# Memory attention one block behind the projections, its tail between the gates of the merge stage: a hybrid gMLP decoder layer on eight cores

## The chip, the cores and the metric

The kernel runs on all 8 cores of one Trainium2 chip: two dies of four cores, cores 0 to 3 and 4 to 7. Each core computes one prompt sequence of 2048 tokens and 16 of the 128 sample sequences (128 tokens); the cores exchange nothing. The metric is the time of the slowest core in microseconds (us). So a change helps only as far as it helps the core that ends last.

Engines as the profile names them: PE is the matrix engine, PEld its weight loads, DVE is VectorE, ACT is ScalarE, POOL is GpSimd, SP issues most DMAs. PEclk is the share of full clock that PE was granted.

## The reference, cut to what matters

```python
h = rmsnorm(x, g_mix)
u, v, p, q, gate_logits = split(h @ w_in)
vhat = layernorm(gelu(v), g_v, b_v)
a = chunk_spatial_gate(gelu(u), vhat, w_s, b_s) @ w_out_a     # within chunks of 128 tokens
b = multiscale_pool(p, ...) @ w_out_b
c = memory_attend(q, mem_k, mem_v) @ w_out_c                  # 4 heads, 256 memory tokens
g_a, g_b, g_c = split(sigmoid(gate_logits))
x = x + (g_a * a + g_b * b + g_c * c) @ w_o
x = x + square(relu(rmsnorm(x, g_ffn) @ w_up)) @ w_down
# outputs: y = rmsnorm(x, g_final), memory k and v, the pooling state, and
# the vhat rows of the last chunk (prompt) and of the sample
```

Matmul operands are bf16, sums are fp32.

## The kernel before

A small scheduler in the file records every operation with the buffers that it reads and writes, and emits each engine's instructions in the order in which they were recorded. So the order of the Python calls is the order on every engine's queue. A buffer comes from a ring; an engine that wants one waits for its last readers. There are 8 PSUM banks in one ring (`pb`), 7 tiles `fA` (`tA`), 4 tiles `fW` (`tW`), and 4 tiles each in the rings for x and for normalised x.

The front works block by block (512 tokens): `Q`, `V`, `P` are projections, `S(j, hp)` the attention scores and their Exp, `AV(j, hp)` the attention output (with Ln and Exp for the division), `WIN` the pooling windows, `U` and `MIX` the spatial gate. `T` transposes, `N` normalises, `vout(i)` writes the normalised v rows. `SA1`, `SA2`, `SA2b`, `SA3` are the same attention for a group of 4 sample sequences, each step waiting for the one before. In the kernel before, all this belongs to block `j` itself:

```python
for j in range(1, 4):
    Q(j)
    ...                                   # V(j) with norms of the next block
    S(j, 0); S(j, 1)
    if j >= 2: SA1(g0); SA1(g1)
    for i in range(4): P(BT[j][i]); vout(i)
    if j == 3: flush(); P(16); vout(4)    # token tile 16 is the sample
    if j >= 2: SA2(g0); SA2(g1)
    if j == 3: load_next("mrg1"); load_next("mrg2")
    WIN(j)
    ...                                   # SA2b, WIN(4), AV(j,0), AV(j,1), T, SA3
    us = [U(j, g) for g in range(4)]      # j == 3: U4() before
    for g in range(4): MIX(j, g, *us[g])
```

`vout(i)` writes the normalised v rows. For the last prompt tile (15) and the sample (16) they are also an output, scaled with gain and bias.

```python
if t >= 15:
    (g0, g0_b), (g1, g1_b), (g2, g2_b) = [tS(t) for _ in range(3)]
    s.dma("sp", [(g0[:], gbv[0:512].partition_broadcast(128))], ...)       # gain
    s.dma("sp", [(g1[:], gbv[512:1024].partition_broadcast(128))], ...)    # bias
    TS("dve", g2[:], gv[:], *sc, ...)
    TT("pool", g2[:], g2[:], g0[:], ALU.mult, ...)
    TT("pool", g2[:], g2[:], g1[:], ALU.add, ...)
    store([(cvo[...], g2[:])], ...)       # issued by the next flush()
```

`MIX` ends on GpSimd as well: `TT("pool", apre[...], tm, ug, mult)`. Then the merge: for each of 8 slices of 128 output channels and 5 column ranges, three gates (24 matmuls, Sigmoid), the three branch products (8 matmuls), and the sum. After it come the output projection, the MLP and the final norm; the change does not touch them.

The softmax here doesn't subtract the row's maximum and nothing guards it: scores larger than these inputs give would overflow.

Of the kernel before, what the change touches and what calls it, by code (L numbers as in the profile page):

```python
# [7 lines left out]
F32 = mybir.dt.float32  # L8
# [178 lines left out]
def build_program():  # L187
# [30 lines left out]
    with st, nc.allow_non_contiguous_dma(reason="small strided rows"), \  # L218
# [14 lines left out]
        def Xt(t):  # L233
# [26 lines left out]
        kvs = [CRf[:, i * 4096:(i + 1) * 4096] for i in range(2)]  # L260
        kvs_b = [[s.buf("kvs%d_%d" % (i, a)) for a in range(2)] for i in range(2)]
        probs = CRf[:, 8192:12288].rearrange("p (a c) -> p a c", a=8)
        probs_b = [s.buf("probs%d" % i) for i in range(8)]
        hmT = CRf[:, 8192:10240].rearrange("p (k c) -> p k c", k=8)
        hmT_b = probs_b[0:4]
        qbd = CRf[:, 12288:13312].rearrange("p (f b c) -> p f b c", f=2, b=16)
        qbd_b = s.buf("qbd")
        prt = [CRf[:, 13312 + i * 512:13824 + i * 512] for i in range(5)]
        prt_b = [s.buf("prt%d" % i) for i in range(5)]
        bnds = CRf[:, 15872:17408]  # L270
        bnds_b = s.buf("bnds")
        cr_old = [(i * 4096 + a * 2048, i * 4096 + a * 2048 + 2048, kvs_b[i][a]) for i in range(2) for a in range(2)] + \
                 [(8192 + i * 512, 8704 + i * 512, probs_b[i]) for i in range(8)] + [(12288, 13312, qbd_b)] + \
                 [(13312 + i * 512, 13824 + i * 512, prt_b[i]) for i in range(5)] + [(15872, 17408, bnds_b)]
# [133 lines left out]
        def norm_load(t, src):  # L408
            xt, xb = ring("xst", xst, xst_b)
            s.dma("sp", [(xt, src)], writes=[xb], owner=xb)  # L410
            norm_src[t] = (xt, xb)
# [291 lines left out]
        def AV(j, hp):  # L703
# [12 lines left out]
            rd, rd_b = tA()  # L716
# [10 lines left out]

        def SA1(g):
# [6 lines left out]
            pr, pr_b = tW()  # L735
# [40 lines left out]
        def mem_loads():  # L776
            gt, gt_b = ring("xst", xst, xst_b)
            s.dma("sp", [(gt, gvec[1].partition_broadcast(128))], writes=[gt_b], owner=gt_b)
# [4 lines left out]
            return gt, gt_b  # L783
# [32 lines left out]
        def load_x(ts):  # L816
            for t in ts:
                norm_load(t, xrow(t))
# [5 lines left out]
        st_ = {}  # L824
        for i in range(4):
            st_[i] = norm_a([i])
            norm_b(*st_[i])
            if i == 2:
                load_next("pq", after=[x_b[2]])
            if i >= 1:  # L830
                N(i - 1)
                T(i - 1)
        N(3)
        load_next("u", after=[slot_b[0]])
        s.dma("sp", [(bnd[:, B_CUR:B_SC], cb[:, B_CUR:B_SC])], writes=[bnd_b], owner=bnd_b)
        gm, gm_b = mem_loads()
        load_x([4, 5, 6])
        setup_loads()
        vmm(0)
        T(3)  # L840
        for i in range(1, 4):
            vmm(i)
        vfin()
        load_next("kv", after=[slot_b[1]])
        Q(0)
        for i in range(4):
            vout(i)
        mst = norm_a([100, 101])
        norm_b(*mst)
        for i in range(4):  # L850
            P(i)
        norm_c(100, gm, gm_b)
        norm_c(101, gm, gm_b)
        load_x([7])
        WIN(0)
        for t in range(2):
            trans(100 + t, hmT, hmT_b, t * 128, "dve")
# [8 lines left out]
        KV()  # L866
        load_next("mrg0")
# [4 lines left out]
        S(0, 0)  # L872
        S(0, 1)
        T(4)
        N(6)
        T(5)
        N(7)
        load_x(BT[2])
        hst = hist_loads()
        AV(0, 0)  # L880
        T(6)
        AV(0, 1)
        T(7)
        hist_ops(*hst)

        for j in range(1, 4):
            nx = BT[j + 1] if j < 3 else []
            g0, g1 = 2 * (j - 2), 2 * (j - 2) + 1
            Q(j)
            vt = BT[j] + ([16] if j == 3 else [])  # L890
            vmm, vfin, vout = V(vt)
            if j == 1:
                na = norm_new(4)
            for i in range(len(vt)):
# [366 lines left out]
```

## Time and profile before

984.55 us, median of 4 runs (984.16 to 987.75).

| stage | core 4 | core 6 | what limits it |
|---|---|---|---|
| to the first setup matmul | 56.9 us | 56.8 us | DMA of x and weights, 97% busy from 25 us on |
| from there to the merge | 134.5 us | 144.3 us | PE, with waits and with half clock |
| merge, to the output projection | 236.1 us | 236.3 us | PE without a gap |
| the rest | 545.2 us | 545.0 us | PE |
| of the time before the merge at half clock | 17.0 us | 34.0 us | follows from the waits |

The span of each core of the profiled run; its clock is the mean share granted to PE:

```profile
core 1: 994.5 us, clock 0.957
...
core 4: 972.7 us, clock 0.989
...
core 6: 982.4 us, clock 0.981
```

Cores 0 and 1 ran most of the front of this one execution at a clock of 0.81; core 6 is the better guide to the timed runs. Busy times of core 6 in three stretches (columns: stretch, length, then PE, PEld, DVE, ACT, POOL busy with the number of instructions, clock, DMA share, GB/s):

```profile
25.00:57.00 32.00, 27.40 (x211) 15.71 (x214) 17.45 (x34) 11.29 (x22) 4.82 (x7) 1.00 0.97 228
57.00:201.10 144.10, 122.01 (x1007) 71.54 (x1015) 81.35 (x164) 68.73 (x126) 32.51 (x34) 0.88 0.41 90
201.10:437.40 236.30, 236.29 (x1298) 126.08 (x1297) 71.67 (x136) 64.82 (x121) 96.72 (x92) 1.00 0.32 66
```

Most of PE's slack is in the second stretch: 22 us without a matmul, and a mean clock of 0.88 (the first has 4.6 us without one). The merge has none. The largest waits of PE from 57 us on, core 6 (total us, times, longest):

```profile
PE bank L341 <- ACT CR L347: 5.6, 3, 2.6
PE bank L341 <- DVE hT L365: 3.6, 2, 2.7
PE bank L344 <- ACT fA L347: 2.8, 1, 2.8
```

The first is the scores waiting for Exp: ScalarE has to load another function table (1.28 us) first. And one view that the prediction did not use, GpSimd near the end of the front on core 6:

```profile
185.88 1.27 POOL L350 TENSOR_TENSOR X<-X 128x512 f32<-128x512 f32 x1 [10.64 <-DMA X<-gbv]
...
197.51 1.26 POOL L350 TENSOR_TENSOR X<-X 128x512 f32<-128x512 f32 x1 [8.19 <-DMA X<-gbv]
198.98 1.27 POOL L350 TENSOR_TENSOR X<-X 128x512 f32<-128x512 f32 x1 [0.20 <-PE bank L341]
200.19 1.70 POOL L156 DMA_DIRECT2D slot<-wpk  x3
202.43 4.96 POOL L350 TENSOR_TENSOR X<-fA 128x512 bf16<-128x512 f32 x4 [0.55 <-DVE fA L359]
```

GpSimd stands still for 10.6 and 8.2 us for the gain and bias loads (`gbv`). It is free again at 201.9 us; for the mix products (the last line) it then waits 0.55 us for VectorE. So no time is lost here, but there is only half a microsecond of slack.

### The profile page before, as it was taken

The page shows a single profiled execution, that of the slowest core. Times are in us where ns is not written, and L with a number is a line of the kernel's source. Part 1 is how long each engine was busy: PE and PEld are TensorE (multiplying, and loading weights), DVE is VectorE, ACT ScalarE, POOL GpSimd, SP SyncE. Part 2 cuts the span into 40 slices and gives each one's busy share as a digit, 9 for nine tenths or more (in the row PEclk, how much of TensorE's full clock was granted, in tenths as well). Part 3 has the DMA queues.
Part 4 walks back from the last instruction along what each step waited for, and adds up shares of the span by engine and source line. Part 5 has one row for each costly group of instructions (what it writes and reads, how often), then busy time and mean ns, then how long its engine had stood idle before and what let it go on. Part 6 is the DMA issues. An engine that isn't in the chain of part 4 may idle for free.

```text
span 994.5 us, 15569 instructions; the slowest of 8 cores (972.7 to 994.5 us)
## 1 busy us (share of the span) xinstructions
PE 941.2 (95%) x5312; PEld 485.5 (49%) x5312; DVE 384.4 (39%) x644; ACT 291.1 (29%) x523; POOL 268.0 (27%) x274
## 2 busy tenths in 40 slices
PE   0878899899999999999999999999999999999996
PEld 0553555455555555554555544455445544455442
DVE  2644665432322233225541234322442224421476
ACT  2255542432222222223553300133002320033332
POOL 2130132143344334434333210133002220023243
PEclk9977778789999999999999999999999999999998
DMA  9954813078122221128023040400404022040034
GB/s 206 208 133 125 177 36 65 24 140 232 38 43 43 43 43 19 25 43 232 1 34 74 1 85 1 85 1 1 85 1 85 2 42 44 5 81 1 35 157 169
DMA packets 16969, 71.26 MB, mean 72 GB/s; under 512 B 2029, under 2 KB 3052, under 8 KB 13052
## 3 DMA queue, kind: packets, MB, share of 16 engines
q0 software_dynamic: 5472, 35.65, 21.1%
q1 hardware_dynamic: 11420, 34.61, 10.3%
q8 instruction: 44, 0.72, 0.3%
q14 instruction: 33, 0.27, 0.1%
HBM read 95.80 MB, written 10.22 MB: 107 GB/s over the span
## 4 chain that ended last, share of the span: by engine, by line
PE 91%; DMA 4%; DVE 1%; SPq 1%; ACT 1%; issue 1%; POOL 0%; DVEq 0%; POOLq 0%; ACTq 0%
PE bank L341 89%; DMA CR<-wpb 2%; DMA X<-x 2%; PE bank L344 2%; SPq L156 1%; DVE X L359 0%; ACT L347 0%; DVE hT L365 0%; ACT fA L347 0%; DVEq L128 0%; ACT CR L347 0%; ACT X L347 0%; DVE fA L359 0%; POOL stats L350 0%; POOL X L350 0%
## 5 line engine op out<-in xcount | busy, mean ns | idle before, releaser
L341 PE MATMUL bank<-hT,slot 128*128 128x436 bf16 (+3 forms) x2480 | 474.3, 352 | 3.4 <-DVE hT L365 3.4
L341 PEld LDWEIGHTS bank<-hT,slot 128*128 128x128 bf16 x2480 | 242.2, 99 | 221.8 <-issue 24.7
L341 PE MATMUL bank<-slot,CR 128*128 128x512 bf16 (+1 forms) x1376 | 298.9, 378 | 0.0
L347 ACT ACTIVATE fA<-bank 128x436 f32<-128x436 f32 (+2 forms) x219 | 119.0, 545 | 385.8 <-PE bank L341 372.1
L341 PEld LDWEIGHTS bank<-slot,CR 128*128 128x128 bf16 x1376 | 134.2, 98 | 157.2
L359 DVE SCALAR_TENSOR_TENSOR X<-bank,stats,X 128x512 f32<-128x512 f32 x136 | 102.1, 750 | 119.7 <-PE bank L341 119.7
L347 ACT ACTIVATE fW<-bank 128x436 f32<-128x436 f32 (+3 forms) x107 | 56.7, 532 | 175.5 <-PE bank L341 174.5
L350 POOL TENSOR_TENSOR CR<-fA 128x436 bf16<-128x436 f32 (+1 forms) x69 | 66.5, 964 | 108.6 <-ACT fA L347 104.6
L350 DVE TENSOR_TENSOR fA<-bank,fA 128x436 f32<-128x436 f32 (+1 forms) x77 | 43.0, 605 | 106.1 <-PE bank L341 102.7
L350 DVE TENSOR_TENSOR CR<-fA 128x436 bf16<-128x436 f32 (+1 forms) x51 | 31.2, 612 | 116.0 <-ACT fA L347 116.0
L350 POOL TENSOR_TENSOR stats<-stats,cstt 128x1 f32<-128x1 f32 (+3 forms) x30 | 35.7, 1189 | 130.4 <-DVE stats L356 99.8
L156 POOL DMA_DIRECT2D slot<-wpk x30 | 17.2, 573 | 182.8 <-PE bank L341 174.6
L341 PE MATMUL bank<-slot,hT 128*128 128x512 bf16 (+1 forms) x272 | 57.8, 384 | 2.6 <-ACT CR L347 2.5
L347 ACT ACTIVATE CC<-X 128x1024 bf16<-128x1024 f32 x34 | 35.9, 1057 | 76.1 <-DVE stats L356 36.8
L341 PE MATMUL bank<-X,slot 128*128 128x436 bf16 (+1 forms) x240 | 57.2, 347 | 0.0
L350 POOL TENSOR_TENSOR CR<-fW 128x436 bf16<-128x436 f32 (+1 forms) x37 | 35.1, 948 | 63.0 <-ACT fW L347 61.5
L350 DVE TENSOR_TENSOR fW<-bank,fW 128x436 f32<-128x436 f32 (+1 forms) x43 | 24.2, 605 | 58.8 <-PE bank L341 58.8
L341 PEld LDWEIGHTS bank<-slot,hT 128*128 128x128 bf16 x272 | 30.5, 113 | 28.3 <-issue 21.3
L350 POOL TENSOR_TENSOR fA<-fA 128x436 f32<-128x436 f32 (+1 forms) x22 | 24.3, 1104 | 71.8 <-DVE fA L350 71.8
L350 DVE TENSOR_TENSOR CR<-fW 128x436 bf16<-128x436 f32 (+1 forms) x29 | 17.8, 612 | 66.3 <-ACT fW L347 66.3
L344 PE MATMUL bank<-bnd,X 128*128 128x128 bf16 x152 | 15.1, 262 | 25.4 <-DVE X L359 23.2
L350 DVE TENSOR_TENSOR X<-bank,X 128x512 f32<-128x512 f32 (+1 forms) x35 | 23.9, 684 | 27.6 <-PE bank L344 14.5
(88 smaller groups left out, 495.6 us busy)
## 6 DMA issues: line engine op xcount, KB each, us to landing
slot<-wpk POOLq DMA_DIRECT2D x30, 1024.0 KB, 13.3
X<-x SPq DMA_DIRECT2D x34, 512.0 KB, 16.0
y<-hT SPq DMA_DIRECT2D x17, 512.0 KB, 2.6
CR<-ck POOLq DMA_DIRECT2D x4, 512.0 KB, 7.8
CR<-cv POOLq DMA_DIRECT2D x4, 512.0 KB, 9.7
gb<-gvec SPq DMA_DIRECT2D x3, 512.0 KB, 13.6
CR<-mem SPq DMA_DIRECT2D x2, 512.0 KB, 20.2
X<-gbv SPq DMA_DIRECT2D x4, 256.0 KB, 3.8
```

The lines of the kernel that those rows point to most:

```text
L156: eng.dma_start(out=o_ap, in_=i_ap).then_inc(owner.sem, 16)
L341: s.op("pe", lambda e: e.matmul(out, lhsT=lhsT, rhs=rhs, start=start, stop=stop), R_, W_)
L344: s.op("pe", lambda e: e.transpose(out=out, in_=in_, identity=identb), R_ + [ident_b], W_)
L347: s.op("act", lambda e: e.activation(out=out, in_=in_, func=func, **kw), R_, W_)
L350: s.op(eng, lambda e: e.tensor_tensor(out=out, in0=in0, in1=in1, op=op), R_, W_)
L359: s.op("dve", lambda e: e.scalar_tensor_tensor(out=out, in0=in0, scalar=scalar, in1=in1, op0=op0, op1=op1), R_, W_)
```

## The change

Its intent: in the loop over blocks, the attention of block j-1 runs among the projections of block j, so that Exp and Ln have matmuls to hide behind. Block 3's attention and all of the sample's then have no later block, and go between the gates of the merge. Buffers in the large tile `CR` are laid out anew to allow it, the start is reordered, and x for the residual is loaded later. The core of the diff, with cuts, and condensed to blocks 2 and 3 (block 1 has an order of its own in the file):

```diff
-        load_next("u", after=[slot_b[0]])
-        gm, gm_b = mem_loads()
-        load_x([4, 5, 6])
-        setup_loads()
-        vmm(0)
+        load_x(BT[1], after=[slot_b[1]])
+        setup_loads()
+        mem_loads()
+        load_next("u", after=[slot_b[0]])
...
         for j in range(1, 4):
-            Q(j)
-            S(j, 0)
-            S(j, 1)
+            S(j - 1, 0)
+            P(BT[j][0]); P(BT[j][1]); Q(j)
+            S(j - 1, 1)
+            P(BT[j][2]); P(BT[j][3])
+            AV(j - 1, 0)                  # j == 3: Q(4), P(16) here
+            AV(j - 1, 1)
             vmm, vfin, vout = V(vt)
...
+            if j == 3:
+                load_next("mrg1")
+                load_next("mrg2")
+            for i in range(4):
+                vout(i)
             WIN(j)
             if j == 3:
                 WIN(4)
+                flush()
+                vout(4)
+                u4 = U4()
...
+        fill = {
+            (0, 0): lambda: (S(3, 0), SA1(0)),
+            (0, 1): lambda: (S(3, 1), SA1(1)),
+            (0, 2): lambda: (AV(3, 0, tX), SA2(0), SA2(1)),
+            (1, 0): lambda: (AV(3, 1, tX), SA2b(0), SA2b(1), kvs_load(2), kvs_load(3)),
+            (1, 1): lambda: (SA3(0), SA3(1)),
+            (1, 2): lambda: (SA1(2), SA1(3)),
+            ...
+        }
+        for m, si in seq1b:
+            G(m, si)                      # three gates
+            if (m, si) in fill:
+                fill[m, si]()
+            B(m, si)                      # three branch products
```

More of the change, by code (lines that the diff above doesn't have):

```diff
@@ L258, in build_program @@
         sth_b = s.buf("sth")
-        kvs = [CRf[:, i * 4096:(i + 1) * 4096] for i in range(2)]
-        kvs_b = [[s.buf("kvs%d_%d" % (i, a)) for a in range(2)] for i in range(2)]
-        probs = CRf[:, 8192:12288].rearrange("p (a c) -> p a c", a=8)
-        probs_b = [s.buf("probs%d" % i) for i in range(8)]
-        hmT = CRf[:, 8192:10240].rearrange("p (k c) -> p k c", k=8)
-        hmT_b = probs_b[0:4]
-        qbd = CRf[:, 12288:13312].rearrange("p (f b c) -> p f b c", f=2, b=16)
-        qbd_b = s.buf("qbd")
-        prt = [CRf[:, 13312 + i * 512:13824 + i * 512] for i in range(5)]
-        prt_b = [s.buf("prt%d" % i) for i in range(5)]
-        bnds = CRf[:, 15872:17408]
-        bnds_b = s.buf("bnds")
-        cr_old = [(i * 4096 + a * 2048, i * 4096 + a * 2048 + 2048, kvs_b[i][a]) for i in range(2) for a in range(2)] + \
-                 [(8192 + i * 512, 8704 + i * 512, probs_b[i]) for i in range(8)] + [(12288, 13312, qbd_b)] + \
-                 [(13312 + i * 512, 13824 + i * 512, prt_b[i]) for i in range(5)] + [(15872, 17408, bnds_b)]
+        prt = [CRf[:, i * 512:512 + i * 512] for i in range(5)]
+        prt_b = [s.buf("prt%d" % i) for i in range(5)]
+        bnds = CRf[:, 2560:4096]
+        bnds_b = s.buf("bnds")
+        probs = CRf[:, 4096:8192].rearrange("p (a c) -> p a c", a=8)
+        probs_b = [s.buf("probs%d" % i) for i in range(8)]
+        hmT = CRf[:, 4096:6144].rearrange("p (k c) -> p k c", k=8)
+        hmT_b = probs_b[0:4]
+        gm = CRf[:, 6144:8192].bitcast(F32)
+        gm_b = probs_b[4:8]
+        kvs = [CRf[:, 8192 + i * 4096:12288 + i * 4096] for i in range(2)]
+        kvs_b = [[s.buf("kvs%d_%d" % (i, a)) for a in range(2)] for i in range(2)]
+        qbd = CRf[:, 16384:17408].rearrange("p (f b c) -> p f b c", f=2, b=16)
+        qbd_b = s.buf("qbd")
+        cr_old = [(i * 512, 512 + i * 512, prt_b[i]) for i in range(5)] + [(2560, 4096, bnds_b)] + \
+                 [(4096 + i * 512, 4608 + i * 512, probs_b[i]) for i in range(8)] + \
+                 [(8192 + i * 4096 + a * 2048, 10240 + i * 4096 + a * 2048, kvs_b[i][a]) for i in range(2) for a in range(2)] + \
+                 [(16384, 17408, qbd_b)]
         slots = [sb("slot%d" % i, [128, 4096], BF16) for i in range(4)]
@@ L406, in build_program, with norm_load @@
         norm_src = {}
-        def norm_load(t, src):
+        def norm_load(t, src, after=()):
             xt, xb = ring("xst", xst, xst_b)
-            s.dma("sp", [(xt, src)], writes=[xb], owner=xb)
+            s.dma("sp", [(xt, src)], writes=[xb], owner=xb, after=after)
             norm_src[t] = (xt, xb)
@@ L701, in S, with AV @@
                     ACT(probs[:, i, :], bks[hh][0][:, :], AF.Exp, [bks[hh][1]], [probs_b[i]], scale=0.125)
-        def AV(j, hp):
+        def AV(j, hp, tmp=tA):
             c0, c1 = hcols(j)
@@ L715, in AV @@
                     MM(bd[hh * 64:(hh + 1) * 64, :], ones, probs[:, i, :], mc == 0, mc == 1, [ones_b, probs_b[i]], [bd_b])
-            rd, rd_b = tA()
+            rd, rd_b = tmp()
             ACT(rd[:], bd[:, :], AF.Ln, [bd_b], [rd_b])
@@ L726, in build_program, with tX @@
         samp = {}
+        def tX():
+            xt, xb = ring("xst", xst, xst_b)
+            return xt[:, 0:512], xb
         def SA1(g):
@@ L734, in SA1 @@
                     MM(bk[32 * b:32 * b + 32, 0:256], qbd[:, hp, 4 * g + b, :], K[:, b, hp, :], hp == 0, hp == 1, [qbd_b, kvs_b[i][0]], [bk_b])
-            pr, pr_b = tW()
+            pr, pr_b = tX()
             pr16 = pr[:, :].bitcast(BF16)
@@ L776, in mem_loads @@
         def mem_loads():
-            gt, gt_b = ring("xst", xst, xst_b)
-            s.dma("sp", [(gt, gvec[1].partition_broadcast(128))], writes=[gt_b], owner=gt_b)
+            s.dma("sp", [(gm, gvec[1].partition_broadcast(128))], writes=gm_b, owner=mem_o)
             m32 = kvs[0].bitcast(F32)
@@ L782, in mem_loads @@
                 norm_src[100 + t] = (m32[:, t * 1024:(t + 1) * 1024], kvs_b[0][t])
-            return gt, gt_b
         def KV():
@@ L814, in T, with load_x @@
             trans(t, hT, [hT_b[t]], t * 128, "dve")
-        def load_x(ts):
+        def load_x(ts, after=()):
             for t in ts:
-                norm_load(t, xrow(t))
+                norm_load(t, xrow(t), after)
         def N(t):
@@ L823, in build_program @@
         vmm, vfin, vout = V(BT[0])
-        st_ = {}
+        s.dma("sp", [(bnd[:, B_CUR:B_SC], cb[:, B_CUR:B_SC])], writes=[bnd_b], owner=bnd_b)
         for i in range(4):
-            st_[i] = norm_a([i])
-            norm_b(*st_[i])
-            if i == 2:
-                load_next("pq", after=[x_b[2]])
-            if i >= 1:
-                N(i - 1)
-                T(i - 1)
-        N(3)
-        load_next("u", after=[slot_b[0]])
-        s.dma("sp", [(bnd[:, B_CUR:B_SC], cb[:, B_CUR:B_SC])], writes=[bnd_b], owner=bnd_b)
-        gm, gm_b = mem_loads()
-        load_x([4, 5, 6])
-        setup_loads()
-        vmm(0)
-        T(3)
-        for i in range(1, 4):
-            vmm(i)
+            nb = norm_a([i])
+            norm_b(*nb)
+            if i >= 2:
+                vmm(i - 2)
+            N(i)
+            T(i)
+            if i == 2:
+                load_next("pq", after=[slot_b[0]])
+        load_x(BT[1], after=[slot_b[1]])
+        setup_loads()
+        mem_loads()
+        load_next("u", after=[slot_b[0]])
+        vmm(2)
+        vmm(3)
         vfin()
-        load_next("kv", after=[slot_b[1]])
         Q(0)
         for i in range(4):
+            P(i)
             vout(i)
-        mst = norm_a([100, 101])
-        norm_b(*mst)
-        for i in range(4):
-            P(i)
-        norm_c(100, gm, gm_b)
-        norm_c(101, gm, gm_b)
-        load_x([7])
         WIN(0)
-        for t in range(2):
-            trans(100 + t, hmT, hmT_b, t * 128, "dve")
+        load_next("kv", after=[norm_src[7][1]])
         setup_ops()
@@ L865, in build_program @@
         setup_mm()
-        KV()
-        load_next("mrg0")
         N(4)
@@ L871, in build_program @@
             MIX(0, g, *us[g])
-        S(0, 0)
-        S(0, 1)
-        T(4)
-        N(6)
-        T(5)
-        N(7)
-        load_x(BT[2])
-        hst = hist_loads()
-        AV(0, 0)
-        T(6)
-        AV(0, 1)
-        T(7)
-        hist_ops(*hst)
+            if g in (1, 3):
+                T(4 + g // 2)
+                N(6 + g // 2)
+        load_x(BT[2])
+        mst = norm_a([100, 101])
+        norm_b(*mst)
         for j in range(1, 4):
             nx = BT[j + 1] if j < 3 else []
-            g0, g1 = 2 * (j - 2), 2 * (j - 2) + 1
-            Q(j)
             vt = BT[j] + ([16] if j == 3 else [])
+            if j == 1:
+                P(4)
+                P(5)
+                T(6)
+                norm_c(100, gm, gm_b)
+                T(7)
+                norm_c(101, gm, gm_b)
+                Q(1)
+                for t in range(2):
+                    trans(100 + t, hmT, hmT_b, t * 128, "dve")
+                hst = hist_loads()
+                P(6)
+                KV()
+                load_next("mrg0")
+                P(7)
+                S(0, 0)
+            else:
+                S(j - 1, 0)
+                if j == 2:
+                    na = norm_new(4)
+                    norm_sq(na, nx[0])
+                    norm_sq(na, nx[1])
+                if j == 3:
+                    n16 = norm_a([16])
+                    norm_b(*n16)
+                P(BT[j][0])
+                P(BT[j][1])
+                Q(j)
+            S(j - 1, 1)
+            if j == 2:
+                norm_sq(na, nx[2])
+                norm_sq(na, nx[3])
+                norm_b(*na)
+                N(nx[0])
+            if j == 3:
+                N(16)
+            if j == 3:
+                T(16)
+            if j >= 2:
+                P(BT[j][2])
+                P(BT[j][3])
+            AV(j - 1, 0)
+            if j == 2:
+                N(nx[1])
+                N(nx[2])
+            if j == 3:
+                Q(4)
+                P(16)
+            AV(j - 1, 1)
             vmm, vfin, vout = V(vt)
@@ L898, in build_program @@
                 if j == 2 and i == 0:
-                    norm_sq(na, 12)
-                    norm_b(*na)
-                if j == 2 and i > 0:
-                    N(nx[i])
-            if j == 2:
-                N(nx[0])
+                    N(nx[3])
+                if j == 2 and i >= 2:
+                    T(nx[i - 2])
             vfin()
@@ L907, in build_program @@
                 norm_b(*na)
-            S(j, 0)
-            S(j, 1)
-            if j >= 2:
-                SA1(g0)
-                SA1(g1)
-            for i in range(4):
-                P(BT[j][i])
-                vout(i)
-            if j == 3:
-                flush()
-                P(16)
-                vout(4)
-            if j >= 2:
-                SA2(g0)
-                SA2(g1)
+                hist_ops(*hst)
+                kvs_load(0)
+            if j == 2:
+                load_x([16])
+                kvs_load(1)
             if j == 3:
@@ L925, in build_program @@
                 load_next("mrg2")
+            for i in range(4):
+                vout(i)
             WIN(j)
-            if j == 1:
-                N(nx[0])
-                load_x([16])
-                N(nx[1])
-                load_x([13])
-                kvs_load(0)
-            if j >= 2:
-                SA2b(g0)
             if j == 3:
                 WIN(4)
-            if j == 2:
-                T(nx[0])
-            AV(j, 0)
-            if j == 1:
-                N(nx[2])
-                N(nx[3])
-                load_x([14, 15])
-            if nx:
-                T(nx[0 if j == 1 else 1])
-            if j >= 2:
-                SA2b(g1)
-            AV(j, 1)
-            if nx:
-                T(nx[1 if j == 1 else 2])
-            if j >= 2:
-                SA3(g0)
-            if j == 2:
-                kvs_load(2)
-                kvs_load(3)
-                T(nx[3])
-            if j == 1:
-                kvs_load(1)
-                n16 = norm_new(1)
-                na = norm_new(4)
+                flush()
+                vout(4)
+                u4 = U4()
             us = []
-            if j == 3:
-                u4 = U4()
             for g in range(4):
@@ L966, in build_program @@
                 if j == 1:
-                    if g == 0:
-                        norm_sq(n16, 16)
-                        norm_b(*n16)
-                        N(16)
-                        load_x([12])
-                    if g == 2:
-                        norm_sq(na, 13)
-                    if g in (1, 3):
-                        T(nx[2 + g // 2])
-            if j == 1:
-                norm_sq(na, 14)
-                norm_sq(na, 15)
-                T(16)
-                Q(4)
-            if j >= 2:
-                SA3(g1)
-            if j == 3:
-                WPO(0)
+                    N(nx[g])
+                    if g >= 2:
+                        T(nx[g - 2])
+                if j == 2 and g < 2:
+                    T(nx[2 + g])
+            if j == 1:
+                load_x(BT[3])
             if j == 3:
                 load_next("mrg3")
+                WPO(0)
             for g in range(4):
                 MIX(j, g, *us[g])
+                if j == 1 and g >= 2:
+                    T(nx[g])
             if j == 3:
@@ L1004, in load_X @@
             s.dma("sp", [(Xt(t), xrow(t))], writes=X_b[t] + extra, owner=X_b[t][0])
-        for t in range(8):
-            load_X(t)
         def toks(c0, c1):
@@ L1014, in blks, with G @@
             return [b for r in tab for b in r[c0 // 512:(c1 + 511) // 512]]
-        for m in range(8):
+        sgs_of = {}
+        def G(m, si):
+            wm, wb = slots[slot_of["mrg%d" % m]], slot_b[slot_of["mrg%d" % m]]
+            c0, c1 = SPLITS[si]
+            n = c1 - c0
+            sgs = []
+            for br in range(3):
+                bk, bk_b = pb()
+                for k in range(8):
+                    MM(bk[:, 0:n], wm[:, (k * 3 + br) * 128:(k * 3 + br + 1) * 128], hT[:, k, c0:c1], k == 0, k == 7,
+                       toks(c0, c1) + [wb], [bk_b])
+                sg, sg_b = tF()
+                ACT(sg[:, 0:n], bk[:, 0:n], AF.Sigmoid, [bk_b], [sg_b])
+                sgs.append((sg, sg_b))
+            sgs_of[m, si] = sgs
@@ L1017, in build_program, with B @@
+        def B(m, si):
             wm, wb = slots[slot_of["mrg%d" % m]], slot_b[slot_of["mrg%d" % m]]
             wq, wq_b = wpo[m % 2], wpo_b[m % 2]
-            if m:
-                WPO(m)
-            for si, (c0, c1) in enumerate(SPLITS):
-                n = c1 - c0
-                sgs = []
-                for br in range(3):
-                    bk, bk_b = pb()
-                    for k in range(8):
-                        MM(bk[:, 0:n], wm[:, (k * 3 + br) * 128:(k * 3 + br + 1) * 128], hT[:, k, c0:c1], k == 0, k == 7,
-                           toks(c0, c1) + [wb], [bk_b])
-                    sg, sg_b = tF()
-                    ACT(sg[:, 0:n], bk[:, 0:n], AF.Sigmoid, [bk_b], [sg_b])
-                    sgs.append((sg, sg_b))
-                for br, (src, tab, nk, wl) in enumerate(((apre, apre_b, 4, [wm[:, 3072 + k * 128:3200 + k * 128] for k in range(4)]),
-                                                         (pm, pm_b, 2, [wq[:, k, :] for k in range(2)]),
-                                                         (oT, oT_b, 2, [wm[:, 3840 + k * 128:3968 + k * 128] for k in range(2)]))):
-                    bk, bk_b = pb()
-                    for k in range(nk):
-                        MM(bk[:, 0:n], wl[k], src[:, k, c0:c1], k == 0, k == nk - 1,
-                           blks(tab, c0, c1) + [wb] + ([wq_b] if br == 1 else []), [bk_b])
-                    sg, sg_b = sgs[br]
-                    TT("dve", sg[:, 0:n], bk[:, 0:n], sg[:, 0:n], ALU.mult, [bk_b, sg_b], [sg_b])
-                (a, ab), (b, bb), (c, cb) = sgs
-                TT("pool", a[:, 0:n], a[:, 0:n], b[:, 0:n], ALU.add, [ab, bb], [ab])
-                TT("pool", CR[:, m, c0:c1], a[:, 0:n], c[:, 0:n], ALU.add, [ab, cb], [cr_b[m][si]] + cr_dep(m, c0, c1))
@@ L1044, in build_program @@
-            load_next()
+            c0, c1 = SPLITS[si]
+            n = c1 - c0
+            sgs = sgs_of.pop((m, si))
+            for br, (src, tab, nk, wl) in enumerate(((apre, apre_b, 4, [wm[:, 3072 + k * 128:3200 + k * 128] for k in range(4)]),
+                                                     (pm, pm_b, 2, [wq[:, k, :] for k in range(2)]),
+                                                     (oT, oT_b, 2, [wm[:, 3840 + k * 128:3968 + k * 128] for k in range(2)]))):
+                bk, bk_b = pb()
+                for k in range(nk):
+                    MM(bk[:, 0:n], wl[k], src[:, k, c0:c1], k == 0, k == nk - 1,
+                       blks(tab, c0, c1) + [wb] + ([wq_b] if br == 1 else []), [bk_b])
+                sg, sg_b = sgs[br]
+                TT("dve", sg[:, 0:n], bk[:, 0:n], sg[:, 0:n], ALU.mult, [bk_b, sg_b], [sg_b])
@@ new lines, in B @@
+            (a, ab), (b, bb), (c, cb_) = sgs
+            TT("pool", a[:, 0:n], a[:, 0:n], b[:, 0:n], ALU.add, [ab, bb], [ab])
+            TT("pool", CR[:, m, c0:c1], a[:, 0:n], c[:, 0:n], ALU.add, [ab, cb_], [cr_b[m][si]] + cr_dep(m, c0, c1))
+        fill = {
[5 more added lines that the diff above has]
+            (1, 2): lambda: (SA1(2), SA1(3)),
+            (0, 3): lambda: (SA2(2), SA2(3)),
+            (1, 3): lambda: (SA2b(2), SA2b(3)),
+            (0, 4): lambda: (SA3(2), SA3(3)),
+        }
@@ new lines, in build_program @@
+        rr["f"] = 0
+        seq1b = [(0, 0), (0, 1), (0, 2), (1, 0), (1, 1), (1, 2), (0, 3), (1, 3), (0, 4), (1, 4)] + [(m, si) for m in range(2, 8) for si in range(5)]
+        for m, si in seq1b:
+            if m and si == 0:
+                WPO(m)
+            if (m, si) == (2, 0):
+                for t in range(8):
+                    load_X(t)
+            if (m, si) != (1, 4):
+                G(m, si)
+            if (m, si) in fill:
+                fill[m, si]()
+            if (m, si) == (0, 4):
+                G(1, 4)
+            B(m, si)
+            if (m, si) == (1, 4):
+                load_next()
+                load_next()
+            elif m >= 2 and si == 4:
+                load_next()
```

## The prediction

> What bounds the kernel now. TensorE does: the chain of waits is 91% PE, and the windows view has PE without a gap from the merge stage to the last store (PE busy 238.9 of 238.9 us in the merge, granted clock 1.00). Only the front, before the merge, has slack. I read core 6 (span 982.4 us), because the three timed runs (984.16 to 987.75) fit it; cores 0 and 1 ran the front of the profiled run at a clock of 0.81 and are a worse guide. Its merge starts at 201.1 us: 25 us until the first dense matmul (DMA of x and the first weights), 32 us of first block with DMA engines 97% busy, 22 us (57 to 79) holding setup, memory K/V and block 0's attention, and 122 us for blocks 1 to 3.
>
> The front's loss. The 122 us hold about 101 us of TensorE work at the full-clock durations in the timeline (Q 3.4, V 6.9, scores 1.3, P 3.6, window 1.8, attention output 2.5, U 6.9, mix 1.1, transposes 2.4 us: about 30 a block, plus the sample). The rest is waits (scores -> Exp with a 1.28 us table load -> next matmul, 2.57, 1.54, 1.54 us; transposes and their evictions 2.7, 2.81, 1.87; the sample's chain 2.19) and the clock that follows them: the clock records of core 6 show 0.5 in seven stretches of 3.4 or 6.8 us. The Trainium skill ("TensorE: Matmul & The Clock Gate", Part 1) says that an idle TensorE falls to half clock in windows of about 3.4 us; this trace agrees. The 57 to 79 stretch loses another 9 us.
>
> What the change does. No matmul is removed. Attention of block j-1 runs among Q and P of block j, so Exp and Ln have matmuls to hide behind; V and U stand closer together. About 11 us of TensorE work (block 3's attention 3.8, the sample's 7.5) moves into the merge, where matmuls of the gates (4.6 us a group) cover its evictions. It comes back there as PE time, so only waits and half-clock time are gained. Added: five switches between Sigmoid and Exp in the merge, about 10 table loads of 1.28 us on ScalarE, which is 27% busy there; I expect 2 us of PE stalls. The start loads pq after v, x of block 1 and setup later, memory last: about as many bytes before setup is ready, 0 to 3 us gained.
>
> Sum. Recoverable: about 20 us of blocks 1 to 3 and 9 around block 0. New waits: block 0's scores have nothing between them and their output (about 3.5 us), VectorE chains of norms, mixes and evictions still hold the first transposes and Q(1) (about 8), small ones and remaining half clock (5). Front ends near 180, merge about 11 longer. Net gain about 13 us.
>
> Prediction: 971 us, 8 in 10 within 958 to 981; faster by over 2% 0.28, within 2% 0.69, slower 0.03.
>
> What would show it: merge start 17 to 25 us earlier on undisturbed cores; merge longer by 9 to 14 us with PE busy there still over 98%; waits of PE on the Exp output gone except in block 1; about 20 table loads instead of 10; fewer 0.5 stretches in the front; everything after the merge unchanged.
>
> What would make it wrong: front waits that vanish altogether (gain over 20 us); or bank or ring stalls in the merge, a later setup load, or new waits on VectorE; or the denser front holding the clock at 0.81 longer.

## The result, and the profile after

998.19 us, median of 4 runs (995.89 to 999.99): slower, by a ratio of 1.013 (95% interval 1.0099 to 1.0161). A ratio here is the mean time of one kernel's fast runs over that of the other's of the same rounds, so it is not quite the ratio of the medians quoted.

The front did get shorter: the merge starts at 180.0 to 183.8 us on all eight cores, where before it started at 191.4 to 201.1 us on the cores at full clock. The rest is unchanged (545.1 to 545.4 us on six cores; 547.8 and 547.9 us on cores 4 and 5, with 15.1 us at a clock of 0.81 in it). The merge takes 261.3 to 264.6 us instead of 236. Core 0 in the same stretches as before, the merge cut in two:

```profile
25.00:57.00 32.00, 25.35 (x190) 13.92 (x191) 15.63 (x30) 9.62 (x19) 4.21 (x6) 0.89 0.93 218
57.00:182.10 125.10, 107.42 (x928) 62.72 (x927) 80.26 (x140) 60.95 (x110) 31.79 (x29) 0.96 0.44 97
182.10:215.00 32.90, 18.49 (x103) 8.18 (x101) 5.67 (x14) 13.26 (x23) 11.42 (x10) 0.79 0.58 113
215.00:446.40 231.40, 229.13 (x1300) 121.23 (x1299) 71.93 (x150) 72.41 (x129) 89.57 (x87) 0.99 0.29 60
```

In the first 33 us of the merge PE is busy for 18.5 us, at a clock of 0.79. PE in that stretch (columns: start, length, engine, line, operation, tiles, shapes, count, and in brackets the idle time before it with its releaser):

```profile
182.82 3.85 PE L344 MATMUL bank<-hT,slot 128*128 128x436 bf16 x20
186.60 0.60 PE L344 MATMUL bank<-X,kT_p 64*128 64x512 bf16 x3
199.05 0.58 PE L344 MATMUL bank<-X,kT_p 64*128 64x512 bf16 x1 [11.84 <-DVE fA L362]
200.77 0.62 PE L344 MATMUL bank<-CR 128*32 128x256 bf16 x8 [1.15 <-DVE fW L362]
202.53 1.61 PE L344 MATMUL bank<-X,slot 128*128 128x436 bf16 x4 [1.14 <-ACT fA L350]
...
222.53 1.73 PE L344 MATMUL bank<-hT,slot 128*128 128x436 bf16 x5 [2.16 <-DVE X L353]
```

After the first three gates and three of four score matmuls, PE waits 11.8 us for a PSUM bank that VectorE has to empty. VectorE was not busy:

```profile
181.58 2.06 DVE L362 SCALAR_TENSOR_TENSOR fA<-bank,cstt,CC 128x512 f32<-128x512 f32 x3
198.15 0.75 DVE L362 SCALAR_TENSOR_TENSOR fA<-bank,cstt,CC 128x512 f32<-128x512 f32 x1 [14.51 <-POOL X L353]
```

It empties three of the four mix banks and then wants a tile of the `fA` ring, which GpSimd has not read yet. GpSimd, and the SP queue that issues its loads:

```profile
177.54 1.49 POOL L353 TENSOR_TENSOR X<-X 128x512 f32<-128x512 f32 x1 [0.20 <-POOL X L353]
193.49 1.26 POOL L353 TENSOR_TENSOR X<-X 128x512 f32<-128x512 f32 x1 [14.45 <-DMA X<-gbv]
194.96 1.26 POOL L353 TENSOR_TENSOR X<-X 128x512 f32<-128x512 f32 x1 [0.20 <-POOL X L353]
196.16 0.59 POOL L156 DMA_DIRECT2D slot<-wpk  x1
196.77 4.93 POOL L353 TENSOR_TENSOR X<-fA 128x512 bf16<-128x512 f32 x4
```

```profile
179.12 0.34 SPq L156 DMA_DIRECT2D cvo<-X  x1
179.56 1.10 SPq L156 DMA_DIRECT2D X<-gbv  x2
```

So the chain is: the sample's gain and bias (two loads of 256 KB) are issued at 179.6 us, behind the store of tile 15 that `flush()` put ahead of them; GpSimd resumes 13.9 us later; the mix products stand behind this wait in GpSimd's queue; their tiles are not released; VectorE cannot empty a mix bank; and the scores of block 3, moved to just after the first gates, need that bank. The clock records of this core show half clock from 192.1 to 205.8 us, of which 7.0 us passed in the wait itself, and once more for 3.4 us at 222.8 us after the 2.2 us wait in the last line shown of PE.

In the kernel before the same loads were issued at 191.4 us on core 6, with U (8.9 us) and the mix still to come on PE: 9.7 us before the merge, against 2.5 us here. They were ahead of the merge weights (issued from 200.2 us), not behind them.

### The profile page after: what moved, and what is told of

It is laid out like the page before. It is cut to its first block, busy times and chain, and to the rows that moved or that the text cites. A ratio compares the mean times of both kernels' runs of the same rounds, so it can differ in the third digit from the quotient of the medians.

```text
span 995.8 us, 15542 instructions; the slowest of 8 cores (986.4 to 995.8 us)
## 1 busy us (share of the span) xinstructions
PE 925.1 (93%) x5269; PEld 476.6 (48%) x5312; DVE 386.5 (39%) x644; ACT 300.6 (30%) x531; POOL 268.5 (27%) x274
## 4 chain that ended last, share of the span: by engine, by line
PE 90%; DMA 3%; DVE 3%; issue 2%; ACT 1%; POOL 1%; DVEq 0%; SPq 0%; POOLq 0%; ACTq 0%
PE bank L344 88%; PE bank L347 2%; DMA X<-gbv 1%; DMA slot<-wpk 1%; DVE X L362 1%; DMA X<-x 1%; POOL X L353 1%; DVE X L359 0%; DVE X L368 0%; DVE fA L362 0%; ACT L350 0%; ACT fA L350 0%; ACT CR L350 0%; DVE stats L553 0%; DVE hT L368 0%
## 5 line engine op out<-in xcount | busy, mean ns | idle before, releaser
L344 PE MATMUL bank<-hT,slot 128*128 128x436 bf16 (+3 forms) x2473 | 468.9, 349 | 5.8 <-DVE hT L368 2.5
L344 PEld LDWEIGHTS bank<-slot,CR 128*128 128x128 bf16 x1376 | 134.5, 98 | 159.8 <-issue 8.1
L350 ACT ACTIVATE fW<-bank 128x436 f32<-128x436 f32 (+2 forms) x103 | 54.8, 533 | 172.8 <-PE bank L344 168.6
L344 PE MATMUL bank<-slot,hT 128*128 128x512 bf16 (+1 forms) x268 | 52.9, 355 | 7.7 <-DMA slot<-wpk 3.8
L353 DVE TENSOR_TENSOR X<-bank,X 128x512 f32<-128x512 f32 (+2 forms) x37 | 25.3, 685 | 43.6 <-PE bank L344 23.0
L344 PEld LDWEIGHTS bank<-slot,hT 128*128 128x128 bf16 x272 | 27.4, 104 | 30.3 <-issue 16.4
```

Source lines behind the costliest of these rows:

```text
L344: s.op("pe", lambda e: e.matmul(out, lhsT=lhsT, rhs=rhs, start=start, stop=stop), R_, W_)
L350: s.op("act", lambda e: e.activation(out=out, in_=in_, func=func, **kw), R_, W_)
L353: s.op(eng, lambda e: e.tensor_tensor(out=out, in0=in0, in1=in1, op=op), R_, W_)
```

## The experiments

**Theory A.** The 11.8 us stall and the half clock behind it come from the late `gbv` load. Without it the change is a small gain. **Rival B.** Attention between the gates costs this by itself, through table loads and held banks; the load is only where the waiting happens to show.

The runs came in three sets; chip 10 for the e and g runs and chip 9 for the f runs. When the e runs were made, one die was at a lower clock in nearly every run, of the kernel before too, so only the undisturbed die is compared (its cores still spent one to five stretches at 0.81, given below where it matters). The f and g runs give ratios.

### e1, g1: no second load

The sample reuses the gain and bias tiles that tile 15 has loaded.

```diff
+                    if t == 15:
                         (g0, g0_b), (g1, g1_b), (g2, g2_b) = [tS(t) for _ in range(3)]
                         ...                       # the two loads
+                        gb_of["v"] = (g0, g0_b, g1, g1_b)
+                    else:
+                        g0, g0_b, g1, g1_b = gb_of["v"]
+                        g2, g2_b = tS(t)
```

> The kernel after, but the sample's normalised v rows are scaled with the gain and bias tiles that token tile 15 already loaded, so the second pair of gbv loads is gone. Theory A (the merge's 11.6 us stall of PE comes from GpSimd sitting behind that late load, and the half clock of 17 us that follows it is part of the bill): stall gone, merge 264 to about 246 us, time 976 to 983. Rival B (the attention between the gates costs this by itself, through table loads and banks): the wait only changes its name, time stays over 990.

e1: 1000.82 us, beside 1004.72 us for the kernel before. On the undisturbed die, the merge took 251.0 to 251.2 us on three cores, with 15.1 us at a clock of 0.81 in it (2.8 us lost), and 252.6 us on the fourth, which had half clock too; 246 us was expected. The cores of that die ended at 980.9 to 983.2 us in the profiled run. The stall is gone. It was repeated later, in a set without a slow die in its runs:

> e1 once more, because its chip held one die in the slow state. Theory A: merge 248 us on undisturbed cores against 261 to 264 of the kernel after, one PE wait of 2.2 us and two of about 1 left; time 0.2 to 0.7% under the kernel before of the same chip. Rival B (the attention between the gates costs by itself): at least as slow as the kernel before.

g1: 980.34 us beside 985.73 us, ratio 0.9936 (0.9888 to 0.9983). One of the six fast runs of the kernel before in this set, 993.95 us, had two cores at a clock of 0.96; without it the ratio is 0.9955, so the gain is 0.4 to 0.6%. The ratios of g2 to g4 have the same base. The merge took 248.3 to 248.5 us on four cores and 250.0 us on the other four, which had 3.4 us of half clock after a wait of 2.16 us that all eight show. Core 0 of g1, front and merge cut as above:

```profile
57.00:182.80 125.80, 109.33 (x922) 64.58 (x929) 80.29 (x140) 62.03 (x111) 34.24 (x31) 0.92 0.41 99
182.80:215.00 32.20, 27.68 (x187) 13.20 (x185) 10.11 (x23) 21.25 (x34) 13.98 (x14) 1.00 0.50 91
215.00:431.30 216.30, 216.17 (x1220) 115.29 (x1218) 67.72 (x141) 64.21 (x118) 84.62 (x82) 1.00 0.31 64
```

The same stretch after the merge start now has PE busy for 27.7 us of 32.2, at full clock. The attention of block 3 and of the sample is still between the gates, so B falls: it does not cost 25 us.

### e2: the load is no longer beside the weights

```diff
-                load_next("mrg1")         # before vout(0)
-                load_next("mrg2")
...
                 vout(4)
+                load_next("mrg1")
+                load_next("mrg2")
```

> The kernel after, but the loads of the second and third merge weights are issued after the sample's gbv loads instead of before. Theory A1 (contention made the gbv load take 13.6 us instead of about 4): the load takes about 4 us again, PE's stall falls from 11.6 to 1 to 3 us, time 980 to 986. If lateness of issue alone counts (A2): stall stays over 8 us, time over 992.

1007.27 us beside 1004.72. GpSimd's wait, core 0 of the kernel after and core 0 of e2:

```profile
POOL X L353 <- DMA X<-gbv: 14.5, 1, 14.5
```

```profile
POOL X L353 <- DMA X<-gbv: 5.4, 1, 5.4
```

Issue to GpSimd's next instruction fell from 13.9 to 4.9 us, so beside two weight loads of 1 MB the same load took 9 us more. PE's longest wait became 2.9 to 3.9 us instead of 8.8 to 11.8, but half clock still followed (6.8 to 10.2 us), and the merge took 257.6 to 260.2 us on cores 0 and 1, 2.8 us of it from 0.81. A1 alone is therefore not the whole: about half of the excess goes. (The edit also puts two more weight issues, 1.1 us, into GpSimd's queue ahead of the mix, so contention's share may be more than this half.) The time expected (980 to 986 us) was missed: the undisturbed die's cores ended at 988 to 997 us.

### e3: the load is issued earlier

```diff
-                flush()
                 vout(4)
+                flush()
```

> The kernel after, but the pending stores are issued after the sample's gbv loads, so these no longer wait in the SP queue behind the store of tile 15. A2 (lateness of issue counts): the loads are issued near 166 us instead of 180.8, before the merge weights, the stall goes, time 976 to 983. A1 (contention alone): they still run beside the merge weights and the stall stays over 6 us, time over 988.

1001.83 us beside 1004.72. The loads were issued at 167 us, directly after tile 15's and before the merge weights, and GpSimd never waits for them (the line is absent from its waits). SP, and the first of GpSimd's two steps on the sample's rows, core 0:

```profile
166.07 1.92 SPq L156 DMA_DIRECT2D X<-gbv  x4
181.97 1.27 POOL L353 TENSOR_TENSOR X<-X 128x512 f32<-128x512 f32 x1 [0.49 <-DVE X L359]
```

The merge took 251.1 us on two cores of the undisturbed die, as in e1, and 252.8 and 253.0 us on the others, where 3.4 us of half clock followed the 2.2 us wait. So early issue is enough to remove the stall. It also avoids the company of the weights, so e3 does not separate the two causes; e2 shows that each has a part. And since e3 loads as many bytes as the kernel after, it is not the bytes saved that helped in e1.

### e4, f3: the same placement in the kernel before

The kernel before, with only the placement of the merge weight loads, `flush()` and `vout(4)` taken from the change.

```diff
-                P(BT[j][i]); vout(i)      # j == 3, four times
-            flush(); P(16); vout(4)
+                P(BT[j][i])               # four times
+            P(16)
+            load_next("mrg1"); load_next("mrg2")
+            vout(0) ... vout(3)
...
+            flush(); vout(4)              # before U4()
             u4 = U4()
```

> The kernel before, with only this one placement taken from the change: second and third merge weights loaded before tile 15's v output, pending stores ahead of the sample's v output, and that output after the window sums. Theory A: the same late load now stalls the old kernel too, somewhere in U or the mix; time 990 to 1002. Rival B: time within 3 us of before, 982 to 988.

e4 gave a wrong result (relative error 1.15): my edit put `P(16)` after the load that overwrites its weight slot. Its time means nothing. Mended:

> The run before this that failed (e4), mended: the sample's pooling projection now stands before the weight load that overwrites its slot. The kernel before with only the placement of the merge weight loads, the pending stores and the sample's v output taken from the change. Theory A: GpSimd sits behind the late gbv load, PE stalls 6 to 12 us between the mix and the first gates, half clock follows, merge start to first output projection or front longer: 10 to 16 us slower than before. Rival B: within 3 us of before.

f3: 990.42 us beside 989.01, ratio 1.0014 (0.9997 to 1.0032). Both expectations of A were missed: PE waits 1.0 to 2.9 us in the merge, not 6 to 12. The trace shows that this run did not make the coincidence. On its core 0 the loads of tile 15 are issued at 181 us and run beside the weights (10 us); the sample's come at 194.8 us, after the weights have landed, and take under 7 us. GpSimd's mix products start 6.7 us after the merge start there, as in e2 (6.7 us), and PE's wait is as in e2 or shorter. So f3 says that these statements alone, in the kernel before, do not cost; that the stall needs the rest of the change as well agrees with this, but was not shown by adding it piece by piece.

### f1: the kernel after as control

> The kernel after, unchanged, as the control for the runs beside it on this chip. Both theories: merge 261 to 265 us on cores at full clock, with PE waits of 9 to 12 us near 190 us; time 12 to 18 us over the kernel before on undisturbed cores.

f1: 1000.87 us beside 989.01, ratio 1.0123 (1.0104 to 1.0142). Waits of 8.6 to 10.9 us in the merge, as before. The result holds in a second set of runs.

### f2: attention of block 3 back before the merge

As e1, but block 3's attention and the first two sample groups run before the first gates.

```diff
-            (0, 0): lambda: (S(3, 0), SA1(0)),
-            ...                           # to (1, 1)
+        S(3, 0); S(3, 1); SA1(0); SA1(1)
+        AV(3, 0, tX); SA2(0); SA2(1); AV(3, 1, tX); SA2b(0); SA2b(1)
+        kvs_load(2); kvs_load(3); SA3(0); SA3(1)
         for m, si in seq1b:
```

> The kernel after without the second pair of gbv loads (as e1), and block 3's attention and the first two sample groups' attention put back before the merge; the other two sample groups stay between the gates. Theory A: the placement between the gates hides 8 to 10 us of waits (Exp table, softmax chain, copies), so this is 5 to 10 us slower than e1's 977 to 983 us on undisturbed cores: merge starts 14 to 18 us later than e1's 182 to 184 and is 7 to 9 us shorter. Rival B (placement between the gates costs more than it hides): this is as fast as e1 or faster.

f2: 992.97 us beside 989.01, ratio 1.0038 (1.0018 to 1.0058). The merge starts at 194.0 to 199.8 us, and took 237.8 us on the one core without half clock or 0.81 in it. The merge ends at 434.9 us there; in f4 (below), same chip, at 426.9 and 429.6 us on the two cores without lowered clock in the merge. The placement between the gates hides 5 to 8 us, of which the f4 edit itself is about 2.5 us (by g1 and g2). Rival B falls a second time: without this placement the change is a loss.

### f4: the attention output after the branch products

As e1, with `AV(3, .)` behind `B` of the same step, against the wait of 2.16 us.

```diff
-            (0, 2): lambda: (AV(3, 0, tX), SA2(0), SA2(1)),
+            (0, 2): lambda: (SA2(0), SA2(1)),
...
+        fill_after = {(0, 2): lambda: AV(3, 0, tX), (1, 0): lambda: AV(3, 1, tX)}
...
             B(m, si)
+            if (m, si) in fill_after:
+                fill_after[m, si]()
```

> As e1, and block 3's attention outputs in the merge are issued after the branch products of their step instead of before. Theory: the 2.2 us wait of PE on VectorE near 208 us (a PSUM bank held through Ln, Exp and the multiply) goes, with the half clock stretch behind it on some cores; merge 2 to 4 us shorter than e1's 248.2 (251.0 with 2.8 us of lowered clock). Rival (the wait is ScalarE's table loads and moves elsewhere): merge within 1 us of e1.

f4: 984.38 us beside 989.01, ratio 0.995 (0.9928 to 0.9973). The 2.2 us wait is gone, and on cores without lowered clock the merge takes 245.8 and 246.0 us, 2.3 to 2.5 less than the best cores of g1 (g2, on g1's chip, repeats it: 245.8 to 246.0 us). The bank that held `AV`'s sum was waited for while Ln (behind a table load), Exp and a multiply ran; with the branch products ahead, the next gates come first.

### g2, g3, g4: the start and VectorE

g2 mends the start as well. In the kernel after, `vmm(0)` was recorded before `N(2)`, so VectorE had to do the statistics of the first v output, which wait for the v weights, before it could normalise tile 2.

```diff
-            if i >= 2:
-                vmm(i - 2)
             N(i)
             T(i)
+            if i >= 2:
+                vmm(i - 2)
...
-        load_x(BT[1], after=[slot_b[1]])
+        load_x(BT[1], after=[slot_b[0]])
```

> As f4, with the start mended: norm and transpose of the third and fourth token tiles are issued before the first v outputs, and the second block's x is loaded once the v weights have landed. Theory C (in the kernel after, VectorE holds the norm of tile 2 behind the statistics of the first v output, which waits for weights: two PE waits of 3.2 us): these waits go, setup matmuls start near 52 us instead of 56 to 60, merge starts 3 to 5 us earlier, time 3 to 5 us under f4. Rival D (the DMA engines bound the start): setup matmuls wait for the same bytes, merge start within 1.5 us of f4's.

g2: 973.63 us, ratio 0.9864 (0.9817 to 0.991). Setup matmuls start at 53.4 to 56.5 us (g1: 55.5 to 59.8), the merge at 177.5 to 181.2 us (g1: 180.5 to 184.8). Against g1 on the same chip this is 6.7 us less, 2.5 in the merge (f4's edit) and some 4 at the start. Theory C is right in the time gained, but its mechanism is not shown: the setup did not start near 52 us, and PE still waits 3.1 us for tile 2 and 4.2 us for tile 3 on core 0. The two edits at the start were not tried apart.

g3 puts six transpose evictions on ScalarE, four of the second block and two of the memory. Two of its edits:

```diff
-                T(4 + g // 2)
+                trans(4 + g // 2, hT, [hT_b[4 + g // 2]], (4 + g // 2) * 128, "act")
...
-                    trans(100 + t, hmT, hmT_b, t * 128, "dve")
+                    trans(100 + t, hmT, hmT_b, t * 128, "act")
```

> As g2, with six transpose evictions of the second block and of the memory on ScalarE instead of VectorE. Theory E (VectorE is the limit between 57 and 79 us, 16.6 us busy of 22, ScalarE 4.6): the four PE waits there (7.3 us in sum) fall by 3 us or more. Rival: ScalarE's eviction is slower and the waits only change their name; merge start within 1 us of g2's.

g3: 971.88 us, ratio 0.9848 (0.98 to 0.9895). The merge starts at 175.1 to 179.9 us, some 2 us earlier than in g2. But PE's waits in the 24 us from the setup's start sum to 6.2 to 8.9 us over the cores, against 7.4 to 9.1 us in g2, and fell by 3 us on none: the mechanism of theory E was missed, and where the 2 us come from stays open.

g4 moves two transposes behind other matmuls.

> As g3, with two transposes moved behind matmuls that need nothing (tile 16's and the third block's first), against PE waits of 2.2 and 1.8 us. Expected: merge starts 2 to 4 us earlier than g3's, time 1.0 to 1.5% under the kernel before and so below both kernels.

g4: 972.57 us, ratio 0.9858 (0.9796 to 0.992). The time is in the range expected, but the merge does not start 2 to 4 us earlier than in g3 (175.1 to 180.7 us): that expectation was missed. g3 and g4 cannot be told apart. Both beat the kernel before and the kernel after.

## Why the prediction was wrong

1. **"The front's loss" and its bound: right.** The merge starts earlier because waits and half clock shrank and work moved. From setup to merge it took 134.5 to 144.3 us before (full-clock cores) and 125.0 to 126 us after. PE's waits for the Exp output in that time fell from 5.6 us on core 6 to 2.0 to 3.6 us over the cores.
2. **"Front ends near 180": right** (180.0 to 183.8 us). "17 to 25 us earlier" holds only against the slow cores of before; against the fast ones (191.4 us) it is 8 to 11 us.
3. **"0 to 3 us gained" at the start: zero** (55.0 to 58.8 us after, 56.3 to 58.0 before). The reorder brought a new order on VectorE, which g2 mended.
4. **"I expect 2 us of PE stalls" in the merge: the step that failed.** Measured on core 0 of the kernel after: waits of 11.84, 1.15, 1.14 and 2.16 us, 16.3 us in sum, and half clock for 13.7 (7.0 of it inside the first wait) and 3.4 us. PE was busy for 93.7% of the merge (18.49 + 229.13 of 264.3 us), not over 98%. Without the stall (g1, core 0) the merge is 15.8 us shorter: 12.1 us fewer waits, and the rest half clock. The moved work was sized too high: about 11 us were expected, but at full clock PE was busy for 243.85 us of g1's merge (27.68 + 216.17), 7.6 us more than before (236.29). With 4.5 us of waits, g1's merge is 12.2 us longer than before, near the "about 11 longer" only because two errors nearly cancel: work too high, stalls too low. (In g2, with 2.4 us of waits left, it is 9.9 us.) The long stall was not in the prediction's sum; it named bank or ring stalls only as a general risk. It was there to be read in the trace before: GpSimd waited 8.2 us for the same loads, with half a microsecond of slack behind it. The change moved P, block 3's attention and the sample's steps away from between v and the mix: from v's statistics on GpSimd to the merge start it was 27 us before (174.1 to 201.1 us, core 6) and 10 us after (172.2 to 182.1 us, core 0), and the weight loads came ahead of the sample's.
5. **The base was a slow core.** The sum was made on core 6 (982.4 us), as if the others gained alike. With the stall mended (g1), all cores end between 975.4 and 980.6 us; before, on the same chip, a fast run's cores ended between 971.4 and 983.4 us in four of its six fast runs. Both medians are near 977.5 us. So the mended change gives the median core nothing, and its 0.6% comes from the core that would have ended last. A change that I expected to bring 13 us brings 5 when its mistake is undone. Of the 27 us between the 13 us expected and the loss of 13.6 us measured, some 16 are thus the stall with its half clock; g1 still lacks some 8 us of the 13, which this base explains at least in part.
6. "About 20 table loads instead of 10": 18 against 10 on the slowest core, and they did no harm that the runs show except the held bank of f4. "Everything after the merge unchanged": right, 545.1 to 545.4 us where the clock was not at 0.81.

What stays open: why the cores of one run of the kernel before differ by up to 17 us in half-clock time although they run the same program, which of the two start edits of g2 counts, and where g3's 2 us come from.

## What to carry to other kernels

When work is moved away from between a load and its use, list every load whose wait was just covered by that work, also on engines that look idle: a GpSimd wait of 8 us that cost nothing before became an 11.8 us stall of the matrix engine. On a machine with in-order queues, a side output (here, two small tiles of gain and bias) should be fetched early or reused, not issued behind a store or beside bulk weight loads. And when the metric is the slowest core, size a gain on the spread of the cores, not on one of them.

## What the Trainium skill lacked or had wrong

- "TensorE: Matmul & The Clock Gate", Part 1, says that a die goes to 13/16 of the clock once three of its cores run dense matmuls, and holds it while the load lasts (on the default power profile; no run shows which one this chip has). Here the clock records of all eight cores of g1 have no 0.81 at all (core 0 from 215 us on, shown above: 1.00). In other runs 0.81 came in stretches of about 2 to 15 us, and in the profiled run before two cores had it for 148 and 131 us in sum between 55 and 217 us. The measurement decides: in this kernel's fast runs it is not the normal state.
- The same part has idle windows of about 3.4 us. The half-clock stretches are multiples of that (3.4, 6.8, 13.7 us), which agrees. But 3.4 us of half clock also followed a wait of only 2.16 us, on four cores of g1 and not on the other four. The part has full clock return after at least one busy window; here PE resumed at 199.05 us after the 11.84 us wait and had full clock at 205.8 us, 6.8 us later, with two waits of over 1 us in between. It says that the window runs free and that the same kernel varies with it; here core 4 and core 6 of one run of the kernel before spent 17.0 and 34.0 us of the front at half clock, and no run shows whether the window's phase is the cause.
- "ScalarE: Activation LUTs", What ACT_TABLE_LOAD costs, gives 1283 ns for the load, as measured here (18 loads, mean 1283 ns), and a drain of about 1380 ns with it. In the kernel after, on core 4, a load from 201.50 us takes 1.28 us and the next activation starts at 202.80 us; the next load starts 0.01 us after the activations end. No drain is seen.
- "Trainium Kernel Development and Optimization", Key Constraints, says that DMAs of all issuing queues share the same 16 engines. e2 agrees and gives the price that the page lacks: a load of two times 256 KB took 4.9 us alone and 13.9 us beside two weight loads of 1 MB from another queue.
